# FF1's products in the order 7, 3, 4; the last block's parts written straight into operand buffers; GpSimd in program order; later gate sums; a rearranged end

## The chip, the core and the metric

The kernel runs on one core of a Trainium2 chip. The metric is the device time of one execution in microseconds (us). Names of engines: PE is TensorE (matmuls), DVE is VectorE, ACT is ScalarE, POOL is GpSimd, SP is SyncE, which only issues DMAs. A name with a q at its end (SPq, POOLq) is the queue in which an engine waits for semaphores and issues DMAs.

## The reference

One decoder layer on 512 tokens of width 2048: a mixing part with two groups of recurrent heads, and a squared-ReLU feed-forward part of width 8192, each between RMS norms and modulated by a conditioning vector `c`. Nearly all of the change lies in the feed-forward part:

```python
h = rmsnorm(x, pre_ffn_norm[l]) * (1.0 + sc_f) + sh_f
y = jnp.square(jax.nn.relu(h @ w_ff1[l])) @ w_ff2[l]
x = x + gt_f * rmsnorm(y, post_ffn_norm[l])
```

`gt_f` is a slice of `silu(c) @ w_ada + b_ada`. The inputs are float32 and results must be near float32.

## The kernel before

**Precision.** Each float32 operand is split into a rounded high part and a rest: ACT casts the tile to the high part (line 247, `wh`), DVE subtracts it from the tile (line 249, `wl`). Line 369 multiplies high by high, low by high and high by low.

**FF1** (h @ w_ff1) goes over 16 blocks of 512 columns. Block 0 is plain (`ff1_plain`). Blocks 1 to 15 (`ff1`) use a scheme of seven products on quarters of the operands in place of eight. The table `ORDER` says in which order the products come: 1, 2, 5, 6, 3, 7, 4. A product has two units `u` (two halves of its columns), each with its own weight tile of 128x1024 and 24 matmuls of 128x256. Three kinds of PSUM banks collect them: px takes products 1, 6, 7, 4 on top of one another, py takes 5 and 3, pz takes 2. After products 1, 5, 6 ACT copies the bank's state out (line 1817, `e`); after 2, 7, 3 DVE adds bank and copy into the result (line 1823); after 4 ACT reads the bank. So a product that adds to a bank must wait until the state of the product before it on that bank was read. Each unit asks the weight stream for its tile (`ws.get`), which splits some units ahead. 

**Weight sums.** Where a product needs a sum of weight quarters, the stream makes it in place: by a DMA from POOL's queue that accumulates (line 264), by a POOL addition or by a DVE addition (both line 269). `WAYS1` says which: POOL for product 5's, DVE for product 7's, DMA for the others. For FF2 POOL makes two sums for each weight tile row (`first_sums`), in buffers `raw` and `n2x`.

**Parts.** After a block, the four result quarters (`G`) and four differences of them (`S`, made by `g_sums`) are squared-ReLU values of hidden units; these seven operands of FF2 are split (`g_split`) and stored to DRAM (`g_store`, tensor `gd`). For block 15 `g_last1` and `g_last0` do that with buffers of their own.

**FF2** goes over 8 chunks of two blocks, (0, 1), (2, 3) to (14, 15), and two halves `m` of the output columns: seven products each with 24 matmuls of 128x512, in `ORDER2` (1, 2, 6, 5, 7, 3, 4), in the very last job in `ORDER3` (1, 2, 6, 5, 3, 7, 4). `load_c` brings a product's operand from `gd` into one of nine buffers (hA, hB and cx, those of FF1's own operand). A product's first weight tile meets the chunk's first block, the second tile meets the second. The banks are qx, qy, qz, with the same rule of succession; results gather in `Y`.

**The end.** In the last job `hook` squares and weighs the tokens' rows as their quarters become final (`weigh`: ACT squares, POOL or DVE multiplies by the gate row `Gf`), takes the norm (`norm`) and adds the residual: `add_norm` on DVE (line 1946) with a store from SP, `add_far` with an ACT scaling (line 1951) and an accumulating DMA on POOL's queue (line 1952), whose store from SP waits in a list until `flush` (line 1958).

**Gate sums.** While the mixing part ends, 64 steps gather the feed-forward gate: POOL accumulates tiles of `w_ada` times `c` into `aaccf` (line 1371); four times, when 512 columns are complete, `total_of` splits the accumulator (ACT line 498, DVE line 499, tile `gsplit`) and sums it over the partitions by two matmuls into `pgf`.

**What sets the order.** Within `manual_schedule` the named engines run in the order of the code; on the others a scheduler with estimated costs places each instruction. In FF1 and most of FF2 only PE and SP are named, so DVE, ACT and POOL may take later work earlier; in the last job all are named.

Of the kernel before, what the change touches and what calls it, by code (L numbers as in the profile page):

```python
# [95 lines left out]
ORDER = (1, 2, 5, 6, 3, 7, 4)  # L96
ORDER2 = (1, 2, 6, 5, 7, 3, 4)
ORDER3 = (1, 2, 6, 5, 3, 7, 4)
# [196 lines left out]
def hybrid_layer_kernel(  # L295
# [57 lines left out]
    CHUNKS = [(r, r + 1) for r in range(0, NR, 2)]  # L353
# [142 lines left out]
    def total_of(ps, a, aH, aL):  # L496

        nc.scalar.copy(out=aH, in_=a)
        nc.vector.tensor_tensor(out=aL, in0=a, in1=aH.bitcast(F32), op=ALU.subtract)
        mm(ps, onesr, aH, True, False)  # L500
        mm(ps, onesr, aL, False, True)
# [843 lines left out]
    def ada_gtf():  # L1345
# [3 lines left out]
        def finish(cb, acc):  # L1349
            cs = slice(cb * 512, (cb + 1) * 512)  # L1350
            wp = ada_tile(f"wpostf{cb}")
            nc.sync.dma_start(out=wp[0:1, :], in_=post_ffn_norm[0:1, cs])
# [4 lines left out]
            nc.sync.dma_start(out=gfd[0:1, cs], in_=wp[0:1, :])  # L1357

        for i in range(len(seq) + LOOK):
# [3 lines left out]
            if i >= LOOK:  # L1363
# [4 lines left out]
                if r == KT - 1:  # L1368
# [3 lines left out]
                    late.append((i + 4, cb, acc))  # L1372
            if late and i >= late[0][0]:
                finish(*late.pop(0)[1:])
            yield
        for e in late:
            finish(*e[1:])
# [225 lines left out]
    with ExitStack() as st:  # L1603
# [68 lines left out]
        def split_to(src, H, L):  # L1672
            nc.scalar.copy(out=H.bitcast(F32R), in_=src)
            nc.vector.tensor_tensor(out=L.bitcast(F32R), in0=src, in1=H, op=ALU.subtract)  # L1674
# [14 lines left out]
        def g_last1():  # L1689
            G = gslots(NR - 1)  # L1690
            parts[(NR - 1, 1)] = []
            for u, (h, lo) in enumerate(((1, 9), (3, 12), (15, 13))):
                split_to(G[:, 1 + u : 2 + u], Yv[:, h : h + 1], Yv[:, lo : lo + 1])
                parts[(NR - 1, 1)] += [(4 + u, 5 + u, 0, Yv[:, h : h + 1]), (4 + u, 5 + u, 1, Yv[:, lo : lo + 1])]

        def g_last0():
            G = gslots(NR - 1)
            Ss = [Yv[:, 8], G[:, 1], Yv[:, 11], G[:, 3]]
            nc.vector.tensor_tensor(out=Ss[0], in0=G[:, 3], in1=G[:, 0], op=ALU.subtract)
            nc.vector.tensor_tensor(out=Ss[2], in0=G[:, 1], in1=G[:, 0], op=ALU.subtract)  # L1700
            nc.vector.scalar_tensor_tensor(out=Ss[1], in0=Ss[0], scalar=-1.0, in1=G[:, 1],
                                           op0=ALU.mult, op1=ALU.subtract)
            nc.vector.scalar_tensor_tensor(out=Ss[3], in0=Ss[1], scalar=-1.0, in1=G[:, 2],
                                           op0=ALU.mult, op1=ALU.subtract)
            Hs = [stage(f"sH{u}").rearrange("p (s j n) -> p s j n", s=2, j=2) for u in range(2)]
            for u, v in enumerate(Ss):
                split_to(v, Hs[u // 2][:, u % 2], v)
            parts[(NR - 1, 0)] = [(0, 2, 0, Hs[0]), (2, 4, 0, Hs[1])]
            for u, n in enumerate((8, 5, 11, 7)):
                parts[(NR - 1, 0)].append((u, u + 1, 1, Yv[:, n : n + 1]))  # L1710
# [68 lines left out]
        def ff1(r):  # L1779
# [3 lines left out]
            for idx, i in enumerate(ORDER):  # L1783
# [6 lines left out]
                if r == NR - 1:  # L1790
# [3 lines left out]
                    if idx in (1, 3, 5, 6):  # L1794
                        load_c(0, {1: 0, 3: 1, 5: 2, 6: 3}[idx])
                    if idx == 6:
                        g_last1()
# [30 lines left out]
                elif i == 4:  # L1828
                    squared(G[:, 0])
            if r == NR - 1:  # L1830
                g_last0()
                return
# [7 lines left out]
        def load_c(c, n):  # L1840
# [7 lines left out]
            for d, r in enumerate(CHUNKS[c]):  # L1848
                nc.sync.dma_start(out=v[:, :, 2 * d : 2 * d + 2, :].rearrange("p h j n -> p h (j n)").bitcast(F32),
# [5 lines left out]
        def at_step(c, m, idx):  # L1855
            if (c, m) == (0, 0):
                if idx == 0:
                    load_c(0, 4)
                elif idx == 1:
                    load_c(0, 5)  # L1860
                elif idx == 2:
                    load_c(0, 6)
                elif idx == 3:
                    g_store(NR - 1, 1)
                elif idx == 4:
                    g_store(NR - 1, 0)
                if idx < 4:
                    return
# [73 lines left out]
        def add_norm(tok, q0, q1):  # L1942
# [4 lines left out]
            nc.sync.dma_start(out=ov, in_=yv)  # L1947
# [22 lines left out]
        def hook(c, m, i, tb=None, ps=None):  # L1970
# [26 lines left out]
            if i == 3:  # L1997
# [4 lines left out]
                if tb == 1:  # L2002
                    norm(1)
                    for tok in range(2):
                        add_norm(tok, 0, 2)
                        add_far(tok, 2, 4)
                return True
            if i == 7:
                tok = 2 + tb
                nc.vector.tensor_tensor(out=yv(tok, 3), in0=yv(tok, 3), in1=ps, op=ALU.subtract)  # L2010
# [21 lines left out]
            flush()  # L2032
# [40 lines left out]
```

## Time and profile before

| what | us |
|---|---|
| three runs: median (lowest to highest) | 2577.28 (2574.63 to 2581.98) |
| profiled execution, its own time | 2582.85 |
| its span | 2581.1 |
| PE busy | 2432.9 (94%) |
| POOL busy | 997.1 (39%) |
| last matmul ends, about | 2566 |

The profile is of one execution. A row of waits names the engine, what it was to do, and what ended the wait. A row of the timeline gives start and length from the span's start; in brackets stands the idle time of the engine just ahead. In the windows the clock is the share of TensorE's full clock that was granted. Matmuls overlap: each lasts longer than the distance to the next, so distances are taken from windows.

### The profile page before, as it was taken

How to read it: one execution, taken by the hardware profiler on the slowest of the kernel's cores; microseconds unless marked ns; L12 is line 12 of the kernel's file. 1: busy time of each engine (PE TensorE's matmuls, PEld its weight loads, DVE VectorE, ACT ScalarE, POOL GpSimd, SP SyncE). 2: the span in 40 equal slices, each digit the busy share in tenths (PEclk: the TensorE clock that was granted, in tenths of full speed). 3: DMA queues.
4: the chain of work that ended last, by engine and by line, in shares of the span. 5: the costliest groups of instructions: out<-in, count | busy, mean ns of one | idle time of the engine just before them, and what ended most of it. 6: DMA issues, size and time to landing. Idle time of an engine off the chain costs nothing. (4 is left out here: it accounts for less than half of the span.)

```text
span 2581.1 us, 39457 instructions
## 1 busy us (share of the span) xinstructions
PE 2432.9 (94%) x14763; PEld 2069.6 (80%) x14763; DVE 1919.1 (74%) x2612; ACT 1263.0 (49%) x2013; POOL 997.1 (39%) x721
## 2 busy tenths in 40 slices
PE   5889999998999899999889999999999999999997
PEld 3667777777777678778789999999998888888885
DVE  7997877768586766753777787777777777877876
ACT  5454544544445442564555565565655433333343
POOL 5561244445455450285222121222233534434423
PEclk9899999999999999999999999999999999999999
DMA  8762434444544432575468888887889988898876
GB/s 318 252 203 75 131 119 142 133 157 129 160 151 156 144 122 82 167 261 195 160 209 250 245 231 250 244 248 236 252 251 344 299 267 253 260 289 227 261 233 185
DMA packets 206645, 535.06 MB, mean 207 GB/s; under 512 B 19315, under 2 KB 23781, under 8 KB 205813
## 3 DMA queue, kind: packets, MB, share of 16 engines
q1 hardware_dynamic: 187968, 465.88, 51.9%
q0 software_dynamic: 18288, 66.59, 14.2%
q8 instruction: 116, 1.90, 0.3%
q14 instruction: 77, 0.62, 0.1%
q10 hardware_dynamic: 196, 0.06, 0.0%
HBM read 463.75 MB, written 67.13 MB: 206 GB/s over the span
## 5 line engine op out<-in xcount | busy, mean ns | idle before, releaser
L249 DVE TENSOR_TENSOR wl<-raw,wh 128x1024 fp32r<-128x1024 f32 x457 | 680.9, 1495 | 260.6 <-ACT wh L247 257.6
L247 ACT CAST wh<-raw 128x1024 fp32r<-128x1024 f32 x463 | 484.0, 1049 | 631.7 <-PE pj L369 167.1
L489 POOL TENSOR_TENSOR aacc<-ada,aacc 128x512 f32<-128x512 f32 x180 | 271.7, 1510 | 255.2 <-ACT ada L487 247.8
L369 PE MATMUL pj<-hH,wh 128*128 128x512 f32 x768 | 325.6, 424 | 0.0
L369 PE MATMUL pj<-hH,wl 128*128 128x512 f32 x768 | 304.9, 397 | 3.5 <-DVE wl L249 3.4
L369 PE MATMUL pj<-hL,wh 128*128 128x512 f32 x768 | 303.5, 395 | 0.0
L269 POOL TENSOR_TENSOR raw<-raw,raw 128x1024 f32<-128x1024 f32 x54 | 159.9, 2962 | 251.3 <-DMA raw<-in_w_ff_dram 179.2
L264 POOL DMA_DIRECT2D raw<-in_w_ff_dram x92 | 81.1, 923 | 359.5 <-DVE wl L249 334.9
L369 PEld LDWEIGHTS pj<-hH,wl 128*128 128x128 f32 x768 | 146.2, 190 | 38.3 <-DVE wl L249 5.3
L369 PEld LDWEIGHTS pj<-hH,wh 128*128 128x128 f32 x768 | 147.1, 192 | 28.9
L369 PEld LDWEIGHTS pj<-hL,wh 128*128 128x128 f32 x768 | 147.4, 192 | 23.5
L487 ACT ACTIVATE ada<-ada,c 128x512 f32<-128x512 f32 x240 | 160.6, 715 | 0.6 <-DMA ada<-in_w_ada_dram 0.6
L369 PE MATMUL px<-hA,wh 128*128 128x256 f32 x480 | 137.3, 286 | 11.6 <-DVE Y L1823 8.4
L369 PE MATMUL px<-hA,wl 128*128 128x256 f32 x480 | 136.6, 285 | 2.5 <-DVE wl L249 2.5
L369 PE MATMUL px<-hB,wh 128*128 128x256 f32 x480 | 136.4, 284 | 0.0
L249 DVE TENSOR_TENSOR w<-raw,w 128x1024 fp32r<-128x1024 f32 x59 | 97.4, 1659 | 39.5 <-ACT w L247 38.3
L489 POOL TENSOR_TENSOR aaccf<-ada,aaccf 128x512 f32<-128x512 f32 x60 | 98.6, 1643 | 45.8 <-ACT ada L487 41.0
L478 DVE SCALAR_TENSOR_TENSOR asum<-adas,c,asum 128x256 f32<-128x256 f32 (+1 forms) x150 | 105.2, 713 | 2.4
L369 PEld LDWEIGHTS px<-hA,wh 128*128 128x128 f32 x480 | 92.7, 193 | 13.8 <-ACT wh L247 11.8
L369 PE MATMUL pout<-wh,oH 128*128 128x512 f32 x256 | 102.0, 400 | 1.4 <-DVE aacc L1488 0.7
L247 ACT CAST w<-raw 128x1024 fp32r<-128x1024 f32 x59 | 61.2, 1048 | 85.4 <-DMA raw<-in_w_ff_dram 36.3
L369 PE MATMUL pout<-wh,oL 128*128 128x512 f32 x256 | 101.0, 394 | 0.6 <-DVE oL L1501 0.6
(562 smaller groups left out, 6763.5 us busy)
## 6 DMA issues: line engine op xcount, KB each, us to landing
raw<-in_w_ff_dram SPq DMA_DIRECT2D x233, 512.0 KB, 5.7
raw<-in_w_in_dram SPq DMA_DIRECT2D x128, 512.0 KB, 3.7
ada<-in_w_ada_dram SPq DMA_DIRECT2D x256, 256.0 KB, 3.3
raw<-in_w_ff_dram POOLq DMA_DIRECT2D x92, 512.0 KB, 6.3
adas<-in_w_ada_dram SPq DMA_DIRECT2D x128, 256.0 KB, 4.8
gd<-Y SPq DMA_DIRECT2D x30, 1024.0 KB, 4.8
hA<-gd SPq DMA_DIRECT2D x50, 512.0 KB, 9.6
hB<-gd SPq DMA_DIRECT2D x50, 512.0 KB, 9.2
```

What stands on the lines that cost most here:

```text
L247: self.cast = self.nc.scalar.copy(out=h, in_=raw).ins
L249: eng.tensor_tensor(out=lo, in0=raw, in1=h.bitcast(F32), op=ALU.subtract)
L264: self.nc.gpsimd.dma_start(out=o, in_=src[0], accum_op=ALU.add)
L269: eng.tensor_tensor(out=o, in0=self.raw[src[-1]], in1=self.raw[src[0]], op=ALU.add)
L369: nc.tensor.matmul(ps, lhsT=lhsT, rhs=rhs, start=start, stop=stop, skip_group_check=chain)
L478: nc.vector.scalar_tensor_tensor(out=acc, in0=av, scalar=cv, in1=acc, op0=ALU.mult, op1=ALU.add)
L487: nc.scalar.activation(out=dst[:, s], in_=a[:, s], func=AF.Copy, scale=c2[:, r0 + r : r0 + r + 1])
L489: nc.gpsimd.tensor_tensor(out=acc, in0=a, in1=acc, op=ALU.add)
```

## The change

Six edits:

1. `ORDER` has 7 ahead of 3. 
2. `ORDER3` has 5 ahead of 6.
3. `CHUNKS` pairs block 0 with block 15, then 1 with 2, up to 13 with 14. The parts of block 15 are not stored: `g_last(i)`, called after each product, splits the quarter that is then ready straight into the operand buffers that FF2's first chunk reads; `load_c` skips block 15. FF2's first seven loads move into block 15's products.
4. From FF1's block 1 to FF2's end POOL, too, runs in the order of the code.
5. The gate sums are parted in two: `parts` splits, `finish` multiplies, eight steps later; the split tile has a buffer of its own in place of one in the residual's ring.
6. The end has new places for `add_norm`, `add_far` and `flush`; token 2's far half is added by DVE, and the last pieces are stored from SP's and ACT's queues in turn.

```diff
-ORDER = (1, 2, 5, 6, 3, 7, 4)
+ORDER = (1, 2, 5, 6, 7, 3, 4)
 ORDER2 = (1, 2, 6, 5, 7, 3, 4)
-ORDER3 = (1, 2, 6, 5, 3, 7, 4)
+ORDER3 = (1, 2, 5, 6, 3, 7, 4)
...
-    CHUNKS = [(r, r + 1) for r in range(0, NR, 2)]
+    CHUNKS = [(0, NR - 1)] + [(r, r + 1) for r in range(1, NR - 1, 2)]
...
-        def finish(cb, acc):
...
+        def parts(cb, acc):
...
+            g = mids[0].tile([P, 2, T], F32R, tag="gs", bufs=1, name=f"gsplit{cb}")
+            nc.scalar.copy(out=g[:, 0, :], in_=acc)
+            nc.vector.tensor_tensor(out=g[:, 1, :], in0=acc, in1=g[:, 0, :].bitcast(F32), op=ALU.subtract)
+            return cb, wp, g
+
+        def finish(cb, wp, g):
             ps = bank("wg", f"pgf{cb}")
-            gsplit = mids[0].tile([P, 2, T], F32R, tag="xr", bufs=3, name=f"gsplit{cb}")
-            total_of(ps, acc, gsplit[:, 0, :], gsplit[:, 1, :])
+            total_of(ps, g[:, 0, :], g[:, 1, :])
...
-                    late.append((i + 4, cb, acc))
+                    late.append((i + 6, lambda cb=cb, acc=acc: parts(cb, acc)))
             if late and i >= late[0][0]:
-                finish(*late.pop(0)[1:])
+                got = late.pop(0)[1]()
+                if got is not None:
+                    late.append((i + 8, lambda got=got: finish(*got)))
...
+        def g_last(i):
             G = gslots(NR - 1)
...
+            to = lambda n, v: split_to(v, *(cs_[(0, n)][:, h, 2:4] for h in range(2)))
+            if i == 2:
+                to(1, G[:, 1])
+            elif i == 3:
+                to(2, G[:, 2])
+            elif i == 7:
+                to(4, G[:, 3])
+            elif i == 4:
+                nc.vector.tensor_tensor(out=S[:, 0], in0=G[:, 3], in1=G[:, 0], op=ALU.subtract)
...
+                to(6, S[:, 1])
...
+                to(5, S[:, 0])
...
+                to(7, S[:, 2])
+                to(3, S[:, 3])
...
-                    if idx in (1, 3, 5, 6):
-                        load_c(0, {1: 0, 3: 1, 5: 2, 6: 3}[idx])
+                    for n in {1: (0,), 3: (1, 2), 4: (3,), 5: (4,), 6: (5, 6)}.get(idx, ()):
+                        load_c(0, n)
...
             for d, r in enumerate(CHUNKS[c]):
+                if r == NR - 1:
+                    continue
...
             if i == 7:
                 tok = 2 + tb
                 nc.vector.tensor_tensor(out=yv(tok, 3), in0=yv(tok, 3), in1=ps, op=ALU.subtract)
-                if tb == 1:
+                if tb == 0:
+                    add_norm(1, 0, 1)
+                else:
                     for tok in range(2, 4):
                         weigh(tok, 3, nc.vector)
-                    flush()
+                    add_norm(1, 1, 2)
                 return True
...
-                add_far(tok, 2, 4)
-                add_norm(tok, 0, 1)
+                flush()
                 return True
...
+            add_norm(2, 0, 1)
             norm(tok)
-            add_norm(2, 1, 2)
+            add_norm(2, 1, 2, nc.scalar)
             for q in range(4):
-                add_norm(tok, q, q + 1)
-            flush()
+                add_norm(tok, q, q + 1, (nc.sync, nc.scalar)[q % 2])
+            for q in range(2, 4):
+                add_norm(2, q, q + 1, (nc.sync, nc.scalar)[q % 2])
             return True

         with tc.manual_schedule(engines={ET.PE, ET.SP}):
             ff1_plain()
+        with tc.manual_schedule(engines={ET.PE, ET.SP, ET.Pool}):
             for r in range(1, NR):
                 ff1(r)
```

The first place is DVE in an FF1 block, around products 7 and 4. `py11_0` is product 3's bank, `px11_0` product 7's, units 0 and 1; the L269 rows make sums for the next block's product 7. Before:

```order
L249 TENSOR_TENSOR wl326_16980<-raw262_16522,wh326_16979 128x1024
L1823 TENSOR_TENSOR Y_11762<-py11_0_16855,e11_0_16719 128x256
L249 TENSOR_TENSOR wl327_17011<-raw263_16553,wh327_17010 128x1024
L269 TENSOR_TENSOR raw270_16983<-raw270_16983,raw268_16917 128x1024
L1823 TENSOR_TENSOR Y_11762<-py11_1_16887,e11_1_16720 128x256
L249 TENSOR_TENSOR wl328_17046<-raw256_16127,wh328_17045 128x1024
L269 TENSOR_TENSOR raw271_17014<-raw271_17014,raw269_16948 128x1024
L1823 TENSOR_TENSOR Y_11762<-px11_0_16717,e11_0_16719 128x256
```

The same engine and place in the next block of the changed kernel (there the eviction has line 1825):

```order
L249 TENSOR_TENSOR wl340_17440<-raw268_16982,wh340_17439 128x1024
L1825 TENSOR_TENSOR Y_11762<-px12_0_17181,e12_0_17183 128x256
L249 TENSOR_TENSOR wl341_17471<-raw269_17013,wh341_17470 128x1024
L1825 TENSOR_TENSOR Y_11762<-px12_1_17182,e12_1_17184 128x256
L249 TENSOR_TENSOR wl342_17510<-raw264_16591,wh342_17509 128x1024
L1825 TENSOR_TENSOR Y_11762<-py12_0_17319,e12_0_17183 128x256
L269 TENSOR_TENSOR raw278_17476<-raw278_17476,raw276_17443 128x1024
L249 TENSOR_TENSOR wl343_17541<-raw265_16622,wh343_17540 128x1024
L269 TENSOR_TENSOR raw279_17478<-raw279_17478,raw277_17474 128x1024
L1825 TENSOR_TENSOR Y_11762<-py12_1_17351,e12_1_17184 128x256
```

The evictions of px now stand ahead of both sums; behind the second sum stands an eviction of py.

The second place is POOL at the change from FF1 to FF2. `raw288` and `raw289` belong to block 15's products, `raw298`, `raw301` and `n2x51` to FF2's first ones. Before:

```order
L269 TENSOR_TENSOR raw288_17971<-raw288_17971,raw292_18300 128x1024
L269 TENSOR_TENSOR raw298_18598<-raw298_18598,raw297_18567 128x1024
L269 TENSOR_TENSOR raw289_18002<-raw289_18002,raw293_18331 128x1024
L264 DMA raw288_17971<-in_w_ff1_dram 128x1024
L269 TENSOR_TENSOR n2x51_18827<-raw298_18598,raw296_18432 128x1024
L264 DMA raw289_18002<-in_w_ff1_dram 128x1024
L269 TENSOR_TENSOR raw301_18796<-raw301_18796,raw300_18765 128x1024
```

The same engine and place in the changed kernel:

```order
L269 TENSOR_TENSOR raw288_17974<-raw288_17974,raw292_18365 128x1024
L269 TENSOR_TENSOR raw289_18005<-raw289_18005,raw293_18396 128x1024
L264 DMA raw288_17974<-in_w_ff1_dram 128x1024
L264 DMA raw289_18005<-in_w_ff1_dram 128x1024
L269 TENSOR_TENSOR raw298_18601<-raw298_18601,raw297_18570 128x1024
L269 TENSOR_TENSOR n2x51_18827<-raw298_18601,raw296_18435 128x1024
L264 DMA raw296_18435<-in_w_ff2_dram 128x1024
L269 TENSOR_TENSOR raw301_18865<-raw301_18865,raw300_18834 128x1024
```

FF2's first two sums moved behind both of block 15's sums and both accumulating DMAs.

The third place is DVE in the last job, around products 7 and 4: in the first column L2010 and L2004 evict product 7, L1946 and L1940 add the residual. Before:

```order
L1946 SCALAR_TENSOR_TENSOR Y<-Y,rsf,hA 128x1024
L1946 SCALAR_TENSOR_TENSOR Y<-Y,rsf,hB 128x1024
L2010 TENSOR_TENSOR Y<-Y,qx_1_0_23086 128x512
L2010 TENSOR_TENSOR Y<-Y,qx_1_1_23087 128x512
L1931 TENSOR_TENSOR Y<-Y,Gf 128x512 x2
L2019 TENSOR_TENSOR Y<-qx_1_0_23086,Y 128x512
```

The same engine and place in the changed kernel:

```order
L1940 SCALAR_TENSOR_TENSOR Y<-Y,rsf,hA 128x1024
L2004 TENSOR_TENSOR Y<-Y,qx_1_0_23068 128x512
L1940 SCALAR_TENSOR_TENSOR Y<-Y,rsf,hB 128x512
L2004 TENSOR_TENSOR Y<-Y,qx_1_1_23069 128x512
L1925 TENSOR_TENSOR Y<-Y,Gf 128x512 x2
L1940 SCALAR_TENSOR_TENSOR Y<-Y,rsf,hB 128x512
L2015 TENSOR_TENSOR Y<-qx_1_0_23068,Y 128x512
```

The residual of token 1 (hB) is added in two pieces, one between the two evictions and one behind them.

More of the change, by code (lines that the diff above doesn't have):

```diff
@@ L494, in column_sum, with total_of @@
             mm(ps[s, i, : w.shape[1]], a[:, s], w, start, stop, cost=0.08)
-    def total_of(ps, a, aH, aL):
-        nc.scalar.copy(out=aH, in_=a)
-        nc.vector.tensor_tensor(out=aL, in0=a, in1=aH.bitcast(F32), op=ALU.subtract)
+    def total_of(ps, aH, aL):
         mm(ps, onesr, aH, True, False)
@@ L1347, in ada_gtf @@
         queue, late, acc = [], [], None
-        def finish(cb, acc):
-            cs = slice(cb * 512, (cb + 1) * 512)
+        def parts(cb, acc):
             wp = ada_tile(f"wpostf{cb}")
-            nc.sync.dma_start(out=wp[0:1, :], in_=post_ffn_norm[0:1, cs])
+            nc.sync.dma_start(out=wp[0:1, :], in_=post_ffn_norm[0:1, cb * 512 : (cb + 1) * 512])
+            g = mids[0].tile([P, 2, T], F32R, tag="gs", bufs=1, name=f"gsplit{cb}")
[3 more added lines that the diff above has]
+        def finish(cb, wp, g):
             ps = bank("wg", f"pgf{cb}")
-            gsplit = mids[0].tile([P, 2, T], F32R, tag="xr", bufs=3, name=f"gsplit{cb}")
-            total_of(ps, acc, gsplit[:, 0, :], gsplit[:, 1, :])
+            total_of(ps, g[:, 0, :], g[:, 1, :])
             nc.vector.tensor_tensor(out=wp[0:1, :], in0=ps[0:1, :], in1=wp[0:1, :], op=ALU.mult)
-            nc.sync.dma_start(out=gfd[0:1, cs], in_=wp[0:1, :])
-        for i in range(len(seq) + LOOK):
+            nc.sync.dma_start(out=gfd[0:1, cb * 512 : (cb + 1) * 512], in_=wp[0:1, :])
+        for i in range(len(seq) + LOOK + 7):
             if i < len(seq):
@@ L1362, in ada_gtf @@
                                       5, *seq[i]))
-            if i >= LOOK:
+            if queue and i >= LOOK:
                 cb, r = seq[i - LOOK]
@@ L1673, in split_to @@
             nc.scalar.copy(out=H.bitcast(F32R), in_=src)
-            nc.vector.tensor_tensor(out=L.bitcast(F32R), in0=src, in1=H, op=ALU.subtract)
+            nc.vector.tensor_tensor(out=L.bitcast(F32R), in0=src, in1=H.bitcast(F32), op=ALU.subtract)
         parts = {}
@@ L1687, in g_split @@
             parts[(r, 1)] = [(4, 7, 0, Yv[:, 12:15]), (4, 7, 1, G[:, 1:4])]
-        def g_last1():
+        def g_last(i):
             G = gslots(NR - 1)
[L1691 to L1710, printed above, removed]
@@ L1829, in ff1 @@
                     squared(G[:, 0])
+                if r == NR - 1 and i != 7:
+                    g_last(i)
             if r == NR - 1:
-                g_last0()
                 return
@@ L1855, in at_step @@
         def at_step(c, m, idx):
[L1856 to L1868, printed above, removed]
+            if (c, m) == (0, 0) and idx < 4:
+                return
             if (c, m, idx) == (0, 1, 0):
@@ L1940, in spots, with add_norm @@
             return y2[:, tok, cs], xv, outf[tok * P : (tok + 1) * P, cs]
-        def add_norm(tok, q0, q1):
+        def add_norm(tok, q0, q1, by=nc.sync):
             yv, xv, ov = spots(tok, q0, q1)
@@ L1946, in add_norm @@
             nc.vector.scalar_tensor_tensor(out=yv, in0=yv, scalar=rsf[:, tok : tok + 1], in1=xv, op0=ALU.mult, op1=ALU.add)
-            nc.sync.dma_start(out=ov, in_=yv)
+            by.dma_start(out=ov, in_=yv)
         def add_far(tok, q0, q1):
@@ L2003, in hook @@
                     norm(1)
+                    add_norm(0, 0, 2)
                     for tok in range(2):
-                        add_norm(tok, 0, 2)
                         add_far(tok, 2, 4)
```

9 lines of the change are left out of this document (7 added, 2 removed).

## The prediction

> **What bounds the kernel now.** I read the page first: its span and its busy shares.
>
> ```profile
> span 2581.1 us, 39457 instructions
> PE 2432.9 (94%) x14763; PEld 2069.6 (80%) x14763; DVE 1919.1 (74%) x2612; ACT 1263.0 (49%) x2013; POOL 997.1 (39%) x721
> ```
>
> TensorE (PE) works 2432.9 of 2581.1 us, so only some 148 us of the span can be won without removing matmuls, and the change removes none. What it can do is take idle time of PE away. The second view is therefore the list of waits of PE alone (what it waited for: us in total, times, longest).
>
> ```profile
> PE px L369 <- DVE Y L1823: 8.4, 9, 1.8
> PE px L369 <- DVE wl L249: 6.0, 2, 3.6
> PE px L369 <- ACT wh L247: 3.1, 3, 1.1
> PE pgf L369 <- ACT gsplit L498: 2.6, 2, 2.1
> PE qx L369 <- DVE Y L2010: 2.3, 1, 2.3
> PE pgf L369 <- DVE gsplit L499: 1.3, 3, 0.6
> PE qy L369 <- DVE Y L1921: 1.3, 1, 1.3
> PE qx L369 <- ACT Y L1917: 1.2, 1, 1.2
> ```
>
> Each row belongs to a place that the diff touches (but for the second one's other wait, 6.0 - 3.6 = 2.4 us), and together they hold 26.2 us. That, with what follows PE's last product, is all the change can reach. The third view is PE's busy time over two neighbouring FF1 blocks (stretch, its length, PE busy and its matmuls, granted clock, DMA share, GB/s).
>
> ```profile
> 1724.70:1766.20 41.50, 40.29 (x336) 1.00 0.81 239
> 1766.20:1807.50 41.30, 39.47 (x331) 1.00 0.81 239
> ```
>
> A block has 14 units of 24 matmuls, and 336 of them take 40.29 us: 0.120 us each, 2.88 us a unit. The rest of a block's 41.5 us is one gap. FF1 is thus bound by PE plus one stall for each block.
>
> **Term A, the order 7, 3, 4.** Here is that stall: VectorE's rows (start, length, in brackets the idle time ahead and what ended it) and the matmul behind it.
>
> ```profile
> 1762.59 0.42 DVE L1823 TENSOR_TENSOR Y<-py,e 128x256 f32<-128x256 f32 x1
> 1762.92 1.22 DVE L249 TENSOR_TENSOR wl<-raw,wh 128x1024 fp32r<-128x1024 f32 x1
> 1766.32 1.23 DVE L269 TENSOR_TENSOR raw<-raw,raw 128x1024 f32<-128x1024 f32 x1 [2.18 <-DMA raw<-in_w_ff_dram]
> 1767.46 0.42 DVE L1823 TENSOR_TENSOR Y<-px,e 128x256 f32<-128x256 f32 x1
> 1768.03 0.36 PE L369 MATMUL px<-hA,wh 128*128 128x256 f32 x1 [1.83 <-DVE Y L1823]
> ```
>
> Product 7 has filled bank px. Its eviction (L1823, 0.42 us) stands in VectorE's queue behind a sum for the next block's weights (L269), which waits 2.18 us for its load. Product 4 writes the same bank and waits for the eviction. The nine waits for L1823 are these; the three waits for the ACT cast (3.1 us) come at the same product, right behind the same eviction, so I count them here: 8.4 + 3.1 = 11.5 us in twelve blocks. The changed order puts both evictions of px ahead of the two sums and the two units of product 3 (5.76 us) between 7 and 4. Behind the waiting sums now stand product 3's second eviction and the low half of the next block's first weights. Bank py is next written by product 5, units later. The weights are split two units ahead, 5.76 us; a sum that still waits 2.18 us, with its own 1.23 and the 0.42 + 1.22 behind it, uses 5.05 of them. So the stall should go and nothing is late next: **-11.5 us** (bounds -5.7, if in half the blocks the loads land later still, and -11.5).
>
> A new neighbour comes with it: 7 now follows 6 on px, so ACT must have copied product 6 out.
>
> ```profile
> 1751.83 1.05 ACT L247 CAST wh<-raw 128x1024 fp32r<-128x1024 f32 x1 [1.52 <-PE px L369]
> 1752.78 0.36 ACT L1817 COPY e<-px 128x256 f32<-128x256 f32 x1
> 1754.68 1.05 ACT L247 CAST wh<-raw 128x1024 fp32r<-128x1024 f32 x1 [1.53 <-PE px L369]
> ```
>
> The copy of unit 0 ends at 1753.14; unit 1 ends at about 1754.6, where the next cast is released. ACT's order is cast, copy there as before, so the copy has 1.5 us to spare: cost 0.
>
> **Term B, the seam from FF1 to FF2.** The largest wait of all (3.57 us) stands in block 15. POOL's, VectorE's and PE's rows, and two windows of PE:
>
> ```profile
> 1905.16 9.99 POOL L269 TENSOR_TENSOR raw<-raw,raw 128x1024 f32<-128x1024 f32 x3 [7.70 <-DVE wl L249]
> 1915.71 2.68 POOL L269 TENSOR_TENSOR n2x<-raw,raw 128x1024 f32<-128x1024 f32 x1
> 1903.86 1.22 DVE L249 TENSOR_TENSOR wl<-raw,wh 128x1024 fp32r<-128x1024 f32 x1
> 1909.48 0.41 DVE L1823 TENSOR_TENSOR Y<-pz,e 128x256 f32<-128x256 f32 x1
> 1909.82 3.09 DVE L249 TENSOR_TENSOR wl<-raw,wh 128x1024 fp32r<-128x1024 f32 x1
> 1912.83 6.65 DVE L1674 TENSOR_TENSOR Y<-Y 128x512 fp32r<-128x512 f32 x2
> 1920.67 0.53 PE L369 MATMUL px<-h6H,wl 128*128 128x256 f32 x1 [3.57 <-DVE wl L249]
> 1917.00:1920.60 3.60, 0.10 (x1) 1.00 0.84 172
> 1920.70:1925.10 4.40, 4.40 (x24) 0.61 0.60 101
> ```
>
> While GpSimd (POOL) adds two weight tiles, a VectorE subtraction with both inputs in SBUF takes 3.09 instead of 1.22 us; the eviction, with one input in PSUM, stays at 0.41. Four additions nearly back to back (9.99 + 2.68 us) hold VectorE until product 6 waits 3.57 us. Behind the wait the clock is 0.61, and 24 matmuls take 4.40 us where 24 x 0.120 = 2.88: 1.5 us more. The stall thus costs 3.57 + 1.5 = 5.1 us.
>
> Now the second of these additions (FF2's first) no longer stands between block 15's two; both DMA accumulations come ahead of it too, and its partner with them. FF2's four additions do not vanish: they fall on products 7, 3 and 4. At (3.09 - 1.22) = 1.87 us for each, VectorE still loses up to 7.5 us there. But it loses them spread over six units, 17.3 us, not in one run, and the rounding of block 15's parts is only 512 wide a piece. Bounds: -5.1 us if each is covered, +2.4 (7.5 - 5.1) if each reaches PE in full. I take **-3.6**, leaving two gaps of some 0.75 us, near the first end: POOL adds a pair of tiles in each of the fourteen blocks before too, and PE's list has two waits of px for a low half, this one and one of 6.0 - 3.6 = 2.4 us. [...]
>
> [...]
>
> The parts of block 15 no longer go to DRAM and back.
>
> ```profile
> 1991.01 0.60 ACT L1917 ACTIVATE Y<-qx 128x512 f32<-128x512 f32 x1 [8.57 <-DMA gd<-Y]
> ```
>
> ACT waits there 8.57 us for a store of those parts out of Y; PE waits 1.2 us for it (last of PE's rows above). With no store left: **-1.2** (bounds -1.2 and 0). The rounding itself is as much work as before, and FF2's first three products need block 15's half only with their second weight tile.
>
> **Term C, the gate sums.** ACT's rows before the first of them:
>
> ```profile
> 1110.52 0.72 ACT L487 ACTIVATE aaccf<-ada,c 128x512 f32<-128x512 f32 x1 [6.64 <-POOL aaccf L1371]
> 1111.15 0.60 ACT L498 CAST gsplit<-aaccf 128x512 fp32r<-128x512 f32 x1
> ```
>
> PE came to the product with `gsplit` before POOL's accumulation and the split were done. Eight steps now lie between split and product for the first three; the fourth is drained at the end, with its split right ahead as before, and keeps its waits. PE's rows for pgf hold 2.6 + 1.3 = 3.9 us; I leave 0.7 to the fourth: **-3.2** (bounds -3.9 and -2).
>
> **Term D, the end.** VectorE, PE and the queues at the end:
>
> ```profile
> 2556.43 1.28 DVE L1946 SCALAR_TENSOR_TENSOR Y<-Y,rsf,hA 128x1024 f32<-128x1024 f32 x1
> 2558.16 1.29 DVE L1946 SCALAR_TENSOR_TENSOR Y<-Y,rsf,hB 128x1024 f32<-128x1024 f32 x1 [0.45 <-POOL rsf L465]
> 2559.36 1.28 DVE L2010 TENSOR_TENSOR Y<-Y,qx 128x512 f32<-128x512 f32 x2
> 2560.19 0.47 PE L369 MATMUL qx<-wh,hB 128*128 128x512 f32 x1 [2.26 <-DVE Y L2010]
> 2567.95 0.88 POOL L1952 DMA_DIRECT2D Y<-cx  x1 [1.59 <-ACT Y L1951]
> 2571.39 1.41 DVE L1946 SCALAR_TENSOR_TENSOR Y<-Y,rsf,hA 128x512 f32<-128x512 f32 x2
> 2574.66 0.57 SPq L1958 DMA_DIRECT2D out_dram<-Y  x1
> ```
>
> With 6 between 5 and 3 on the last job's bank qy, the wait of 1.3 us (qy, L1921) has some 5.8 us of matmuls over it (twice FF1's unit) and goes: -1.3. Product 4 waits 2.26 us because the second L1946 (0.45 of waiting and 1.29) stands ahead of L2010. It now stands behind L2010's first half, in two pieces: the eviction can start at 2556.43 + 1.28 = 2557.71 and PE at about 2558.5: -1.7. After PE's end token 2's far half is added by VectorE as two pieces of 0.7 us in place of ACT and a POOL DMA: the last VectorE row ends at 2572.80 - 1.7 + 1.4 = 2572.5, and the last issue, on one of two queues, at about 2573. Before, the last issue began at 2574.66, behind that POOL DMA. So the tail ends some 1.7 to 2.2 us earlier, of which the 1.7 is the stall. I take -1.3 - 1.9 = **-3.2** (bounds -4.5 and -1, for ACT's queue has not issued stores so late in this trace).
>
> **The sum.** -11.5 - 3.6 - 1.2 - 3.2 - 3.2 = -22.7 us. The profiled execution took 2582.85 us, 1.75 more than its span, and 5.57 more than the median 2577.28; 2582.85 - 22.7 = 2560.2 for such an execution, 2577.28 - 22.7 = 2554.6 for the median, where the change is judged. A measurement of this kernel can tell about 0.3%, 7.7 us, from no change.
>
> **Rivals.**
> 1. *The seam gives nothing back.* FF2's additions hold VectorE at products 7 to 4, and PE waits 1.87 us four times: term B is +2.4 for -3.6. For it: the 3.09 us row. Against it: the pairs in fourteen blocks that PE does not feel. Time: 2554.6 + 6.0 = 2560.6.
> 2. *Only half of A goes.* The sum's load lands later when product 7's buffers are freed in another order, and the next block's first weights are late. The 5.05 of 5.76 us leave only 0.7 us. Time: 2554.6 + 5.8 = 2560.4.
> 3. *The stall moves to 6 and 7, and the kernel is slower.* ACT's cast ahead of the copy of product 6 waits for a load in every block:
>
> ```profile
> ACT wh L247 <- DMA raw<-in_w_ff_dram: 84.4, 20, 9.0
> ```
>
> Such waits exist, up to 9.0 us, but 20 in the whole program. The spare is 1.5 us; beyond it each us costs 15 us over the fifteen blocks. From 1.5 + 22.7 / 15 = 3.0 us late the kernel is slower than before; at 3.5 us it takes 2554.6 + 15 x 2.0 = 2584.6.
> 4. *The straight path is late.* FF2's third product needs block 15's differences with its second weight tile: after two FF2 products and a half, each of 24 matmuls twice as wide as FF1's and so some 24 x 0.24 = 5.8 us: 14.4 us. VectorE has nine pieces of 512 there, at 0.7 us (1.41 for two, above), and two weight halves of 1.22: 8.7 us. If they take twice as long, 3 us are lost, at 2557.6: inside the forecast's range.
>
> **Chances.** The forecast with rival 4, 2549 to 2560: 0.70. Rivals 1 and 2 alone or together (up to 2566.4): 0.20. Rival 3: 0.04. A return of nearly nothing, several terms failing at once: 0.06. The range goes from 2547 (every bound on the good side: 22.7 + 1.5 + 0.7 + 1.3 = 26.2, or 2551, and half the spread of the runs shown, 3.7) to 2567 (rivals 1 and 2 together). Faster by over 0.3%, below 2569.6: 0.90; within it 0.06; slower 0.04.
>
> **What would show it.** Right: no wait of px for L1823 in FF1's blocks, and blocks of 40.3 us; no gap over 2 us in block 15 and no clock under 0.9 there; pgf waiting at one place only; product 4's wait for the eviction of product 7 under 1 us at the end, and the last issue within 1 us of VectorE's last row. Wrong: px waiting for ACT's copy of product 6, or for the low half of the next block's first weights; qx of FF2's chunk 0 waiting for a split of block 15.

## The result, and the profile after

The changed kernel takes 2559.38 us (median of six runs, 2555.46 to 2565.96), the kernel before 2579.3 us (six runs, 2574.6 to 2582.43): a ratio of 0.9927, with a 95% interval of 0.9909 to 0.9945. That is 14 to 23 us less. 2554.6 was predicted, in a range of 2547 to 2567. The profiled execution took 2558.09 us.

The page of the changed kernel answers to the one before: a shorter span, and PE busy for 5.5 us less with as many matmuls.

```profile
span 2556.2 us, 39334 instructions
PE 2427.4 (95%) x14763; PEld 2065.9 (81%) x14763; DVE 1959.9 (77%) x2615; ACT 1264.3 (49%) x2012; POOL 992.9 (39%) x720
```

The rows of PE's waits in the changed kernel that answer to those of before, and the new ones among them:

```profile
PE px L369 <- DVE wl L249: 3.3, 3, 2.3
PE pout L369 <- ACT wh L247: 2.2, 2, 1.6
PE qy L369 <- DVE Y L1915: 1.8, 1, 1.8
PE qx L369 <- DVE Y L2004: 1.4, 1, 1.4
PE pout L369 <- DVE wl L249: 1.1, 1, 1.1
PE pgf L369 <- DVE gsplit L1352: 0.2, 1, 0.2
```

Product 4's wait for product 7 is gone from FF1, and of the waits for a low half 1.0 us is left to block 15 (3.3 less the 2.3 at FF1's start). The wait of the gate sums (pgf) has turned into waits of the output projection (`pout`). The wait on qy in the last job, which was to vanish, is longer than the 1.3 us of before.

A clearer account comes from PE's windows over five stages: the output projection with the gate sums, FF1's blocks 1 to 14, block 15, FF2 to PE's end, and what follows PE's last matmul. The kernel before:

```profile
1053.80:1241.30 187.50, 181.61 (x800) 0.98 0.68 230
1317.40:1896.60 579.20, 565.16 (x4705) 1.00 0.82 242
1896.60:1942.10 45.50, 41.93 (x339) 0.96 0.93 280
1942.10:2565.90 623.80, 618.32 (x2690) 1.00 0.85 261
2565.90:2581.10 15.20, 0.01 (x1) 0.61 0.84 250
```

The changed kernel, the same five stages:

```profile
1056.20:1242.00 185.80, 180.10 (x800) 0.99 0.68 232
1317.80:1881.30 563.50, 561.20 (x4704) 1.00 0.83 248
1881.30:1923.10 41.80, 40.75 (x340) 1.00 0.93 278
1923.10:2543.70 620.60, 617.41 (x2690) 1.00 0.84 252
2543.70:2556.20 12.50, 0.05 (x1) 0.70 0.87 302
```

In this pair the stages give -1.7, -15.7, -3.7, -3.2 and -2.7 us, 27.0 in all. The parts outside them took 2.1 us more, and the pair stands 24.9 us apart, 5 more than the medians: two executions are not two medians. The stage that decided it is FF1.

One of the ten executions of the kernel with the gate sums alone (below) took 4778 us; its median counts it, its ratio does not.

### The profile page after: what moved, and what is told of

Its sections match the earlier page's. It is cut to its first block, busy times and chain, and to the rows that moved or that the text cites. A ratio compares the mean times of both kernels' runs of the same rounds, so it can differ in the third digit from the quotient of the medians.

```text
span 2556.2 us, 39334 instructions
## 1 busy us (share of the span) xinstructions
PE 2427.4 (95%) x14763; PEld 2065.9 (81%) x14763; DVE 1959.9 (77%) x2615; ACT 1264.3 (49%) x2012; POOL 992.9 (39%) x720
## 3 DMA queue, kind: packets, MB, share of 16 engines
q0 software_dynamic: 18144, 66.07, 14.1%
## 4 chain that ended last, share of the span: by engine, by line
PE 63%; DVE 6%; ACT 2%; issue 2%; POOL 2%; DMA 1%; POOLq 0%; DVEq 0%; SPq 0%; ACTq 0%
PE qx L369 13%; PE px L369 13%; PE pj L369 10%; PE py L369 7%; PE qy L369 6%; PE pout L369 4%; PE pz L369 3%; PE qz L369 3%; DVE wl L249 1%; POOL aaccf L489 1%; PE pa L369 1%; DMA raw<-in_w_ff_dram 0%; DVE uc L1070 0%; PE p L369 0%; DVE utmp L1068 0%
## 5 line engine op out<-in xcount | busy, mean ns | idle before, releaser
L249 DVE TENSOR_TENSOR wl<-raw,wh 128x1024 fp32r<-128x1024 f32 x457 | 701.8, 1541 | 215.2 <-ACT wh L247 214.0
L269 POOL TENSOR_TENSOR raw<-raw,raw 128x1024 f32<-128x1024 f32 x54 | 161.4, 2989 | 126.5 <-DVE wl L249 68.2
L249 DVE TENSOR_TENSOR w<-raw,w 128x1024 fp32r<-128x1024 f32 x59 | 116.8, 1992 | 26.5 <-ACT w L247 26.5
L369 PE MATMUL pout<-wl,oH 128*128 128x512 f32 x256 | 100.6, 394 | 1.1 <-DVE wl L249 1.1
```

The lines of the kernel that those rows point to most:

```text
L249: eng.tensor_tensor(out=lo, in0=raw, in1=h.bitcast(F32), op=ALU.subtract)
L269: eng.tensor_tensor(out=o, in0=self.raw[src[-1]], in1=self.raw[src[0]], op=ALU.add)
L369: nc.tensor.matmul(ps, lhsT=lhsT, rhs=rhs, start=start, stop=stop, skip_group_check=chain)
```

## The experiments

Each experiment starts from the kernel before or from the changed one and differs in one part. This table has the stage lengths (us) of every profile, read from windows as above, and the medians. The kernel before was measured again beside each group of them, with medians of 2579.35 to 2580.33 us; a ratio is always to the one beside it.

| kernel | projection, gate sums | FF1 1 to 14 | block 15 | FF2 | tail | median |
|---|---|---|---|---|---|---|
| before | 187.5 | 579.2 | 45.5 | 623.8 | 15.2 | 2579.3 |
| order alone | 191.6 | 565.1 | 45.9 | 621.8 | 14.5 | 2570.82 |
| gate sums alone | 185.3 | 573.4 | 45.6 | 624.2 | 15.2 | 2572.58 |
| end alone | 189.6 | 576.6 | 46.5 | 621.2 | 13.6 | 2574.99 |
| POOL's order alone | 188.4 | 575.6 | 40.5 | 632.5 | 15.2 | 2583.05 |
| parts alone | 189.2 | 570.5 | 44.2 | 622.7 | 12.3 | 2571.07 |
| changed | 185.8 | 563.5 | 41.8 | 620.6 | 12.5 | 2559.38 |
| changed, again | 184.1 | 565.9 | 41.3 | 621.4 | 12.4 | 2559.57 |
| changed, multiplications spread | 185.9 | 565.0 | 42.0 | 620.4 | 12.4 | 2556.32 |
| changed without POOL's order | 184.1 | 563.7 | 43.2 | 618.4 | 12.4 | 2554.64 |
| the same, again | 185.0 | 565.3 | 43.2 | 618.7 | 12.5 | 2555.31 |
| the same, eviction first | 185.9 | 567.0 | 43.2 | 617.9 | 13.3 | 2554.61 |
| POOL's order in FF1 only | 184.3 | 565.2 | 41.3 | 618.0 | 12.5 | 2553.59 |

### FF1's order alone

```diff
-ORDER = (1, 2, 5, 6, 3, 7, 4)
+ORDER = (1, 2, 5, 6, 7, 3, 4)
```

> The kernel before with FF1's order alone changed (7 ahead of 3). Theory: each stall at product 4 cost about 0.2 us more than its idle row, since the fourteen blocks took 575.2 us before and 561.1 after the whole change; so the blocks run at 40.1 us each, PE's waits for the eviction of product 7 are gone, and the kernel is 14 us faster (0.9946). Rival 1, the prediction's own price: only the idle rows go, 11.5 us (0.9955). Rival 2: without the other edits the stall comes back at 6 and 7 (PE px waiting for ACT's copy), less than 4 us gained. The wait of 3.6 us in block 15 stays in all three.

Measured: 0.9967 (0.9954 to 0.998), some 8.5 us faster. FF1's window and that of block 15:

```profile
1323.30:1888.40 565.10, 562.69 (x4704) 1.00 0.84 248
1888.40:1934.30 45.90, 42.20 (x339) 0.96 0.92 272
```

All fourteen blocks lose their stall, and nothing comes back at 6 and 7: rival 2 is out. Against the profile of before the stage is 14.1 us shorter. But that profile was the worst of five: the kernels that keep the old order show 579.2, 573.4, 576.6, 575.6 and 570.5, a mean of 575.1, where the eight with the new order stand at 563.5 to 567.0, a mean of 565.1. The order is worth about 10 us in the mean of these executions, and 5 to 14 in single ones. The stall's length differs from profile to profile: PE's waits in px for L1823 (L1827 and L1821 in the second and the last) and for ACT's cast, as the prediction counted them, sum to 11.5, 6.1, 7.9, 8.4 and 6.3 us in these five, and there are none here. VectorE's waits for the load ahead of L269 sum to 43.9 us in the profile of before and to 16.6 us in that of the changed kernel; that the landing of the loads sets the length of each stall is the author's estimate from such rows, not shown. The interval of the times agrees with 10, holds rival 1's 0.9955 barely, and leaves out the theory's 0.9946: right on the cause, wrong on the size.

### The gate sums alone

```diff
-                    late.append((i + 4, cb, acc))
+                    late.append((i + 6, lambda cb=cb, acc=acc: parts(cb, acc)))
...
+                if got is not None:
+                    late.append((i + 8, lambda got=got: finish(*got)))
```

> The kernel before with the gate sums alone parted (edit 5). Theory: pgf's 3.9 us of waits go, but about 3 us come back at the output projection, where PE then waits for ACT's and DVE's split of its weights (0.6, 1.6 and 1.1 us in the whole change): 0 to -1.5 us, not to be told from no change. Rival, the prediction's price: nothing comes back, -3.2 us, and the waits of pout in the whole change are due to something else.

Measured: 0.9975 (0.9962 to 0.9988), some 6.5 us faster (3 to 10 by the interval): more than the theory had, with the rival's 3.2 at the interval's edge. Its waits of PE at the projection, and two rows of ACT there:

```profile
PE pout L369 <- ACT wh L247: 2.2, 2, 1.6
PE pout L369 <- DVE wl L249: 1.5, 2, 1.1
PE pgf L369 <- DVE gsplit L1352: 0.2, 1, 0.2
```

```profile
1111.16 0.72 ACT L487 ACTIVATE aaccf<-ada,c 128x512 f32<-128x512 f32 x1 [6.65 <-POOL aaccf L1373]
1112.29 1.04 ACT L247 CAST wh<-raw 128x1024 fp32r<-128x1024 f32 x1
```

The theory had the waits right: pgf's 3.9 us shrink to 0.2, and 3.7 us come back at `pout`, so idle time is even. ACT still waits 6.65 us for POOL's accumulation, and its cast for `pout` comes behind that. The theory left out the clock. PE's windows over the same 20 us around the first gate sum, in the kernel before, in this one, in the changed kernel and in its second profile:

```profile
1106.00:1126.00 20.00, 17.34 (x63) 0.83 0.86 291
```

```profile
1106.00:1126.00 20.00, 17.29 (x75) 1.00 0.80 270
```

```profile
1106.00:1126.00 20.00, 17.29 (x68) 0.91 0.74 252
```

```profile
1106.00:1126.00 20.00, 17.37 (x75) 1.00 0.81 272
```

PE is busy for the same time in all four, but gets 63, 75, 68 and 75 matmuls done: before, the clock falls behind the waits of 2.1 and 0.6 us, and 0.83 over 20 us is some 7 us at half speed (0.50 over 1111.8 to 1118.6 us). The five kernels with the old gate sums need 187.5 to 191.6 us for this stage (mean 189.3), the eight with the new ones 184.1 to 185.9 (mean 185.1): 4.2 us. Against the profile of before this kernel gains 187.5 - 185.3 = 2.2 us at even idle time: that is the clock. The same windows in all thirteen profiles divide the 4.2 us roughly. Over these 20 us the clock is 0.83 in four of the five old ones and 0.91 in the fifth, 0.91 in three of the eight new ones and 1.00 in five: 2.4 us in the mean. Around the second gate sum, over 1140 to 1156 us, PE is busy for 14.8 us in the mean of the old ones and 15.9 of the new: 1.1 us less idle time.

### The end alone

```diff
-ORDER3 = (1, 2, 6, 5, 3, 7, 4)
+ORDER3 = (1, 2, 5, 6, 3, 7, 4)
...
+                    add_norm(1, 1, 2)
```

> The kernel before with the end alone changed (edit 6 with the last job's order). Theory: the six POOL multiplications of the third product stand in a row and keep DVE's low half from starting for about 8 us, so product 3 still waits about 1.8 us on qy; product 4's wait falls from 2.3 to 1.4 and the time from PE's last matmul to the end of the span from 15.2 to 12.4 us: -3 us. Rival: the long hold of DVE comes with POOL's written order (edit 4), which is not in this kernel; then the wait on qy is gone and the end gains 4.5 to 5 us.

Measured: 0.9981 (0.9971 to 0.999). The rival is right: there is no wait on qy at all here, and product 4's is 0.5.

```profile
PE qx L369 <- issue: 1.3, 2, 0.9
PE qx L369 <- ACT Y L1917: 1.0, 1, 1.0
PE qx L369 <- DVE Y L2010: 0.5, 1, 0.5
```

So the new order of the last job works by itself, and in the whole change something undoes it. The tail is 13.6 us. (With the parts alone, whose end is the old one, it is 12.3: from the end of the last store's issue to the end of the span pass 4 to 6 us, and with the old end the tail differs by up to 3 us between profiles.)

### POOL's order alone

```diff
         with tc.manual_schedule(engines={ET.PE, ET.SP}):
             ff1_plain()
+        with tc.manual_schedule(engines={ET.PE, ET.SP, ET.Pool}):
```

> The kernel before with POOL's order alone written out (edit 4). Theory: FF2's first sum no longer stands between block 15's two, the 3.6 us wait there falls under 1.2 us and the clock stays at full: block 15 is about 5 us shorter, -5 us in all (0.998). Rival: the seam needs the straight path of block 15's parts (edit 3) as well, since POOL's additions meet DVE's splits either way; the wait stays above 2 us and the gain is under 2 us.

Measured: 1.0012 (1.0003 to 1.0021), slower. The windows of block 15 and of FF2, and the waits of PE that are new or longer:

```profile
1894.20:1934.70 40.50, 40.35 (x339) 1.00 1.00 300
1934.70:2567.20 632.50, 621.83 (x2690) 0.99 0.85 259
```

```profile
PE qx L369 <- ACT Y L1917: 4.5, 1, 4.5
PE qy L369 <- DVE Y L1921: 4.0, 1, 4.0
```

The theory holds for the seam: block 15 is 5.0 us shorter, with the clock at full. But two waits in FF2 grow, from 1.2 to 4.5 us and from 1.3 to 4.0, and take back more. FF2 is 8.7 us longer in the pair: 6.0 by these two waits, and PE itself is busy for 3.5 us more for as many matmuls (621.83 against 618.32), with a clock of 0.99 over the stage in place of 1.00; other waits shrink a little. Behind the wait on qy matmuls start 0.43 us apart at 2547.5 us, where they start 0.23 apart ahead of it; where the rest of the 3.5 us fell is not shown. The first is ACT's, held by the same store of block 15's parts as before; edit 3 removes it. ACT's row there:

```profile
1986.95 0.60 ACT L1917 ACTIVATE Y<-qx 128x512 f32<-128x512 f32 x1 [11.87 <-DMA gd<-Y]
```

The second is the wait that the end alone had made vanish.

### The parts alone

```diff
-    CHUNKS = [(r, r + 1) for r in range(0, NR, 2)]
+    CHUNKS = [(0, NR - 1)] + [(r, r + 1) for r in range(1, NR - 1, 2)]
...
             for d, r in enumerate(CHUNKS[c]):
+                if r == NR - 1:
+                    continue
```

> The kernel before with edit 3 alone (blocks paired 0 and 15, block 15's parts straight into operand buffers). POOL's order is still the scheduler's. Theory: the 3.6 us wait in block 15 stays, since it comes from POOL's order; the wait of qx for ACT's L1917 at FF2's start (1.2 us before, 4.5 us with POOL's order alone) goes, because no store of block 15's parts holds Y any more; -1 to -2 us. Rival: the straight splits themselves load DVE and ACT at the seam, block 15 gets longer, and the kernel is not faster.

Measured: 0.9966 (0.9954 to 0.9979). FF1's window and block 15's:

```profile
1319.60:1890.10 570.50, 562.91 (x4704) 1.00 0.84 245
1890.10:1934.30 44.20, 40.95 (x339) 1.00 0.98 293
```

The wait for ACT at FF2's start is gone, as both prediction and theory had it. The stall of 3.6 us has broken into three (0.4, 1.7 and 1.1 us), none of which brings the clock down (1.00 over the block): block 15 is 1.3 us shorter although POOL's order is the old one. The theory, in which the wait of 3.6 us stays and 1 to 2 us are gained, was wrong on both. Some 9 us were gained by the medians; block 15 and FF2 show 2.4 of them. This profile's FF1 stage was also the shortest of the five with the old order; whether edit 3 does that in every execution, or chance did it in this one, is not shown.

### The changed kernel without POOL's order

```diff
-        with tc.manual_schedule(engines={ET.PE, ET.SP, ET.Pool}):
```

> The changed kernel without edit 4 (POOL's order is the scheduler's again up to the last job). Theory: POOL's written order gains about 5 us at the seam and loses about 2 us at the end. So here PE waits about 3.5 us in block 15 with the clock at half behind it, but product 3 of the last job waits for nothing, as in the run with the end alone (product 4: about 0.5 us); 2 to 4 us slower than the changed kernel. Rival: with the straight parts the additions meet other work, the seam is no worse than in the changed kernel, and this one is 2 us faster than it.

Measured: 0.9899 (0.9885 to 0.9912), where the changed kernel on the same chip gave 0.992 (0.9908 to 0.9933): 4.9 us faster by the medians, though the two intervals just overlap. Its windows of block 15 and FF2:

```profile
1875.40:1918.60 43.20, 40.97 (x339) 1.00 0.96 288
1918.60:2537.00 618.40, 617.26 (x2690) 1.00 0.83 252
```

Neither theory had it whole. PE waits 0.5 and 1.7 us in block 15, and the clock stays up (1.00 over the block). With the straight parts in place POOL's order is worth only 1.4 to 1.9 us at the seam (43.2 against 41.8 and 41.3), and it costs 2.2 to 3.0 us in FF2 (618.4 against 620.6 and 621.4). So edit 4 makes the change worse, not better, by about 1 us in these two stages; where the rest of the 4.9 comes from is not shown. Run again, the kernel gave 0.9903 (0.9889 to 0.9916), with the same waits in block 15 and none on qy.

> The changed kernel without edit 4 once more, unaltered, on the same chip as the two others: about 0.990 of the kernel before, no wait on qy in the last job, block 15's waits 2.1 us in sum.

### Shorter rows of multiplications

```diff
-                    for tok in range(4):
+                    for tok in range(2):
                         weigh(tok, 2, nc.gpsimd)
+                elif i == 3:
+                    for tok in range(2, 4):
+                        weigh(tok, 2, nc.gpsimd)
```

> The changed kernel with two of the six POOL multiplications at the last job's products 5 and 6 moved to product 3, so that POOL runs at most four, then two, in a row. Theory: a DVE subtraction with both inputs in SBUF does not begin to move until POOL's row of ready multiplications is over (8.8 us behind six, 5.9 behind four, 3.4 behind two); with shorter rows it ends in time, the 1.8 us wait on qy goes and the 1.4 us wait on qx falls to about 0.5: 2 to 2.7 us faster than the changed kernel. Rival: the wait on qy is set by the order of DVE's own rows (two weight halves ahead of the eviction), and stays above 1.2 us; no gain.

Measured: 0.9908 (0.9893 to 0.9924); the changed kernel beside it 0.992 (0.9908 to 0.9933), not to be told apart. POOL's and DVE's rows in the last job of this kernel:

```profile
2512.67 7.87 POOL L1925 TENSOR_TENSOR Y<-Y,Gf 128x512 f32<-128x512 f32 x6
2512.81 8.81 DVE L249 TENSOR_TENSOR wl<-n,wh 128x1024 fp32r<-128x1024 f32 x1
```

The edit failed to do what it was to do: six multiplications still run in a row, since ACT squares ahead and all of them wait behind the two accumulating DMAs, the first of which in turn waits 4.17 us for DVE. So the run doesn't test the theory by removing the row, but it repeats it: six multiplications, and one subtraction that takes 8.81 us and is followed by a wait on qy of 1.5 us. (The changed kernel's own rows are 7.87 and 8.82 us.) It doesn't decide against the rival either; POOL's order in FF1 only, below, does.

> The changed kernel once more, unaltered, for comparison on the same chip. All theories: 0.9927 of the kernel before within its interval, the same waits in its profile (qy 1.8, qx 1.4, px 0.8 us), FF1's blocks at 40.1 us.

Run again, the changed kernel waits in the same places: 2.5 us on qy (1.8 the first time), 1.4 on qx and 0.4 in block 15 (0.8 the first time).

The other lengths of such rows come from the kernels above. With the end alone, two in a row:

```profile
2540.89 3.21 POOL L1931 TENSOR_TENSOR Y<-Y,Gf 128x512 f32<-128x512 f32 x2
2541.80 3.40 DVE L249 TENSOR_TENSOR wl<-raw,wh 128x1024 fp32r<-128x1024 f32 x1 [0.81 <-ACT wh L247]
```

With POOL's order alone, four in a row:

```profile
2526.46 5.36 POOL L1931 TENSOR_TENSOR Y<-Y,Gf 128x512 f32<-128x512 f32 x4
2527.01 5.90 DVE L249 TENSOR_TENSOR w<-raw,w 128x1024 fp32r<-128x1024 f32 x1 [0.32 <-ACT w L247]
```

In the kernel before, six that came one by one as ACT released them:

```profile
2536.08 10.93 POOL L1931 TENSOR_TENSOR Y<-Y,Gf 128x512 f32<-128x512 f32 x6 [4.78 <-ACT tail L1930]
2538.47 1.66 DVE L249 TENSOR_TENSOR wl<-raw,wh 128x1024 fp32r<-128x1024 f32 x1 [1.85 <-ACT wh L247]
2541.55 4.31 DVE L249 TENSOR_TENSOR w<-raw,w 128x1024 fp32r<-128x1024 f32 x2 [0.22 <-ACT w L247]
```

The subtraction, 1.2 us by itself, ends 1.1 us behind POOL's row in all three (2545.20 and 2544.10, 2532.91 and 2531.82, 2521.62 and 2520.54), so that much of it lies behind the row. Where POOL's multiplications come one by one, the subtractions end while POOL's row still goes on (1.66 us, and 2.15 each).

### POOL's order in FF1 only

```diff
             for r in range(1, NR):
                 ff1(r)
+        with tc.manual_schedule(engines={ET.PE, ET.SP}):
             for c_ in range(len(CHUNKS)):
```

> The changed kernel with POOL's order written out in FF1 alone; in FF2 up to the last job it is the scheduler's again. Theory: the loss of edit 4 lies in the last job only, where the six multiplications pile up behind the two accumulating DMAs; here they stand ahead of these, so qy waits for nothing and the time from FF2's start to PE's end is 618 to 619 us in place of 620 to 621; the seam is as in the changed kernel (its block 15 wait under 1.5 us): 2.5 to 4 us faster than the changed kernel, level with the run without edit 4. Rival: the loss sits in the seam or in the rest of FF2, and FF2 stays at 620 us or more.

Measured: 0.9898 (0.9883 to 0.9913), 2553.59 us beside 2580.33 of the kernel before: the lowest median of all, though its four executions and those of the kernel without edit 4 beside it (2552.28 to 2554.28, 2552.48 to 2556.93) overlap. The windows of block 15 and FF2, and the rows of POOL and DVE in the last job:

```profile
1878.60:1919.90 41.30, 40.72 (x339) 1.00 0.94 279
1919.90:2537.90 618.00, 617.33 (x2690) 1.00 0.83 253
```

```profile
2502.35 11.03 POOL L1925 TENSOR_TENSOR Y<-Y,Gf 128x512 f32<-128x512 f32 x6 [6.42 <-ACT tail L1924]
2513.34 1.21 DVE L249 TENSOR_TENSOR wl<-n,wh 128x1024 fp32r<-128x1024 f32 x1
```

It keeps the seam of the changed kernel and FF2 of the one without edit 4. The theory holds: the six multiplications now stand ahead of the DMAs and come one by one, the subtraction that took 8.8 us takes 1.21, and PE waits no longer on qy and 0.7 in place of 1.4 us on qx. That is 2.5 us or more, all of it in the last job. VectorE's rows around it stand in the same order as in the changed kernel, so the rival of the run before, that this order sets the wait, is out.

### Product 7's eviction first

```diff
                     norm(1)
-                    add_norm(0, 0, 2)
...
                 if tb == 0:
-                    add_norm(1, 0, 1)
+                    add_norm(0, 0, 2)
...
+                    add_norm(1, 0, 1)
```

> The run without edit 4, and in the last job token 0's first residual sum (1.3 us of DVE) moved from ahead of product 7's first eviction to behind it. Theory: product 4's wait (1.1 us) is the time that this sum stands in front of the eviction; it falls to about 0.3 us and the kernel is 0.5 to 1 us faster than the run without edit 4. Rival: the sums that are now later push back the last stores, and the end of the span does not move.

Measured: 0.9903 (0.9889 to 0.9917), as without the edit. PE's window of FF2 and the tail:

```profile
1927.40:2545.30 617.90, 617.23 (x2690) 1.00 0.83 252
2545.30:2558.60 13.30, 0.00 (x0) 0.63 0.87 303
```

Product 4 waits no longer, and FF2 is 0.5 to 0.8 us shorter; the tail is 0.8 us longer. That is as the rival had it: FF2 and the tail together take 631.2 us, against 630.8 and 631.2 without the edit, so PE's gain is handed back in this profile. That the end is a fixed amount of DVE's and the queues' work is argued from it, not shown.

## Why the prediction was right

- **The bound.** Right. Of the 27.0 us that the stages of the pair show, 16.7 came from idle time of PE, 7.6 from PE being busy longer for as many matmuls, some of them at half clock, and 2.7 from the tail.
- **Term A, -11.5 us.** The mechanism held, in every block, and the new neighbour 6 and 7 cost nothing. The term was mis-sized: it was read off one execution, of which the order's worth was 14.1 us (the idle rows, and 2.5 us in which PE was busy longer for as many matmuls, 565.16 against 562.69), while over the five old profiles it is 10.0 us, and 8.5 by the times of the order alone.
- **Term B, -3.6 and -1.2.** The sizes held, as far as these profiles tell: block 15 is 3.7 us shorter in the pair (4.3 by the means of the four profiles that keep both parts of the old seam, 45.9, and of the four that have both parts of the new, 41.6), and the wait for ACT is gone. No run shows that gaps left over in general cost their own length and no more, as the 1.5 us in the first number have it; what the runs showed is block 15 of the changed kernel, with 1.05 us idle, a clock of 1.00 and 40.75 us for 340 matmuls, 0.120 us each. The share was put wrongly. The text laid the first number on POOL's order. That alone gives 5.0 us, the parts alone 1.3, and both about 4.3. The parts hide most of what the order is worth, but without them it meets a store, and PE's wait for that is 3.3 us longer.
- **Term C, -3.2.** The sum is near (1.7 us in the pair, 4.2 by the means), and the step was wrong. Leaving pgf's products for later did not remove the delay: ACT, held up before the split, now has the weights of `pout` late, and PE waits about as long there. What was won is mostly the clock, 2.4 of the 4.2 us, which the text had not counted there; idle time shrank by about 1 us in place of 3.2. That the sum is near is luck.
- **Term D, -3.2.** The failed step is "with 6 between 5 and 3 the wait of 1.3 us goes". It goes with the end alone, and comes back as 1.8 and 2.5 us with POOL's written order, where two DMAs ahead of the multiplications make them one row and hold a weight half for 8.8 us. The text had counted edit 4 at the seam only. The wait for L2010 fell by 0.9 in place of 1.7. The tail made up for both: it was priced at 0.2 us beside the stall, and is 2.7 us shorter in the pair, 1.8 of which pass behind the start of the last issue (6.5 us before, 4.7 after). That, too, is luck.
- **The sum.** -22.7 was predicted, -19 to -21 measured (0.9927, and 0.992 in the second measurement): A is smaller by 1.5 to 3 us, and edit 4 costs 2 to 3 in the last job. That these differences, with C's surplus, make up the rest is arithmetic on means of a few profiles, not shown by one run. So the mechanism of the largest term held, and the total came near because errors of both signs offset each other. The five parts run alone give -8.5, -6.4, -4.9, +3.1 and -8.8 us, -25.5 in all; with intervals of 2 to 3 us to either side of each, that is not clearly apart from the whole.
- **The rivals.** The stall at 6 and 7, the slower side, did not occur. Half of A going would have left waits in FF1's blocks; with the new order no profile has one of more than 0.4 us in blocks 1 to 14 behind FF1's start. The seam that gives nothing back was wrong as well.

What stays open: why block 15 is 1 us longer with POOL's order and the parts together than with POOL's order alone; no run took the parts' splits away there. Open, too, is most of what edit 3 gains by itself and edit 4 costs by the medians.

## What to carry to other kernels

The stalls at product 4 summed to 6.1 to 11.5 us in the five profiles with the old order: take the price of such a stall from several executions, or say that one profile shows one draw. When several edits meet the same engines, a written order that helps at one place (here the seam, 5 us by itself and 1 to 2 with the straight parts) must be followed through to every later place where that engine runs (here the last job, 2 to 3 us lost); limited to the stage it was meant for, it kept the one without the other. And a wait that is moved off an engine's queue without the work behind it coming earlier can show up again at the next instruction of that queue: here pgf's waits fell from 3.9 to 0.2 us, and 3.7 us came back at `pout`.

## What the runs showed of the hardware

Rows of GpSimd multiplications that were ready held a VectorE subtraction with both inputs in SBUF (1.2 us by itself) to their end: it took 3.40, 5.90 and 8.81 us with rows of 3.21, 5.36 and 7.87 us. Not every row does that: between the three additions of 9.99 us in block 15 of the kernel before, which followed each other without a gap, a subtraction got through behind each of the first two, in 3.08 and 3.09 us; the additions themselves took 3.32 to 3.38 us each, the fourth, behind a DMA issue, 2.68. What divides the two cases is not shown. The prediction had bounded the loss at 1.87 us for each addition from that row, and had no row of multiplications.

The granted clock of TensorE went to half behind idle times of 2.06 and 0.60 us with one matmul between them (0.50 from 1111.8 to 1118.6 us in the kernel before), and behind 2.45 us at FF1's start there (0.50 over 3.4 us). Behind 2.30 us at the same place in the changed kernel it was 1.00. With 2.49 us idle in blocks 1 to 14 in the changed kernel without POOL's order, PE was busy for 561.21 us there, as in the changed kernel (561.20); with 2.45 us idle and POOL's order in FF1 only, for 562.75, as many matmuls in all three. At the gate sums, waits of 1.6 and 1.1 us with a matmul between gave 0.91 over 20 us in the changed kernel's first profile; its second had 1.00 there, with PE busy for 17.37 us in place of 17.29. So like idle times left different clocks; what decides it is not shown. FF1's stalls at product 4 in the kernel before, of up to 1.83 us in blocks of 41.5 us, left the clock at 1.00 in every stretch of 10 us from 1330 to 1890 us.
